# A two-block transformer trunk on one core: where the modulation's products are computed, and how they are spread behind the tiles of the first projection

## The chip, the cores and the metric

The kernel runs on one core of one Trainium2 chip. The metric is the device time of one execution in microseconds (us); three executions of the kernel before gave 1600.56, 1601.52 and 1603.43, so 1601.52 is its median.

## The reference, cut to what matters

Two transformer blocks run over 256 tokens of width 2048, in float32. The part that the change touches is the head of the first block:

- `mod = silu(c) @ w_ada + b_ada`: one row vector of 2048 against a 2048 x 6144 matrix. It is split into shift, scale and gate, of 2048 each.
- `h = rms(x) * (1 + scale) + shift`, then `proj = h @ w_in`, 2048 x 8192.
- Attention and a gated recurrence follow, then `x = x + gate * (y @ w_out)`, and then the second block.

So shift and scale of a stretch of 512 columns of `h` must be known before `w_in` can be multiplied with those columns; gate is needed only at the end of the first block.

## The kernel before, in words

**Modulation.** `w_ada` is cut into tiles of 512 rows x 512 columns, 1 MB each: tile (ng, kg) holds output columns 512 ng and up, and rows 512 kg and up. `ada_tile` (line 368) loads one tile by the SP queue (line 372 or 374) and runs its four chunks of 128 rows (line 375): each chunk multiplies a 128x512 block by a column of `cact` and adds it to an accumulator. A plan of four letters says who does each chunk. "V" is one scalar_tensor_tensor on VectorE (line 382; the first one of an accumulator a tensor_scalar, line 380). "P" is a multiplication on ScalarE into a buffer `pts` of two (line 387), and an addition on GpSimd (line 388; the first one only the multiplication, line 384). After the fourth kg, `ada_sum` (line 393) adds up the 128 partitions of each accumulator by matmuls with ones on TensorE, one set for each accumulator of the plan, and VectorE adds the bias (line 399).

**Order.** `ada_steps` (line 402) is a generator that gives one tile at each step. Of a pair of column groups, one of scale (ng 4 to 7) and one of shift (ng 0 to 3), the tiles alternate. The first pair comes in the front, beside the projection of the memory. The other three pairs come in the first three passes over `w_in`, with `PAIR`: all chunks of the scale group by "P", all of the shift group by "V". The four gate groups (ng 8 to 11) come later with `GATES`: three "V" and one "P" in each tile of the first three groups, each gate group with two accumulators and so two sets of matmuls.

**The passes.** The loop at line 833 goes over four row groups kg of `w_in`, and in each over 12 tiles n of 512 x 512. `tile_mm` (line 141) loads a tile into one of three buffers (`wr`, line 108) and does it in two halves of 256 rows. For each half, ScalarE casts it to `wh` (line 121), VectorE writes the difference to `wl` (line 122, two buffers), and TensorE multiplies (line 166). After the matmuls of a half, `drain` gives out queued work, here mostly one evacuation `part` of an earlier tile: on ScalarE in the first pass (line 632), on VectorE in the others (line 634). After the second half, `post` calls `after` (line 811), which advances the modulation by one tile where n is 0, 1, 2, 4, 5, 6, 8, 9 or 10 (the ninth step is the last sum). After n = 11, `make_h` (line 429) builds the next 512 columns of `h` from the pair: four instructions at line 436 and four at line 438 on VectorE, four at line 437 on ScalarE. Pass kg + 1 multiplies with these columns, so it can't begin before them. In the passes `AHEAD` is 0: a half is multiplied as soon as it is split.

**Gates.** In the fourth pass the modulation is advanced at n = 10 only. After it, the linears of lines 891 to 895 advance it after each tile, in `post` (line 190), while the recurrence (line 747) runs beside them on VectorE, GpSimd, ScalarE and TensorE.

**Queues.** Each engine takes its instructions in order; a scheduler of the language puts them in that order at build time, near the written one but not the same. All loads are issued by SP in order. A load waits until its buffer is free, and the loads behind it wait with it. The tiles of `w_ada` in the passes have two buffers of their own (line 365), used in turn; those of the gates share `wr`.

Of the kernel before, what the change touches and what calls it, by code (L numbers as in the profile page):

```python
# [33 lines left out]
BUDGET = dict(mem=0.3, pass0=0.5, pass3=2.0, gz=1.3, az=1.1, out=0.5, in2=0.1, mla=0.9, o=0.6, ffn=0.1, down=0.3)  # L34


GATES = ("VVVP", "VVVP", "VVVP", "VVVV")
PAIR = ("PPPP", "VVVV")

EARLY = 3  # L40
GSTART = 10
# [19 lines left out]
def trunk_kernel(ctx, tc, a, out):  # L61
# [76 lines left out]
        while jobs:  # L138
            jobs.popleft()()

    def tile_mm(src, kc0, kt, cw, mode, banks, act, first, last, pre=None, post=None):

        raw = load(src, kt, cw)
        n = 2 if mode == "N" else cw // P
        nk = 4 if cw == 256 else 2

        def one(kc, b, hi, lo):
            xh, xl, xx = act(kc0 + kc)  # L150
            hi, lo = hi[:, kc % nk, :], lo[:, kc % nk, :]
            st, sp = first and kc == 0, last and kc == kt - 1
            if mode == "T":
                o = banks[b // 2][:, (b % 2) * T : (b % 2) * T + T]
                s = slice(b * P, b * P + P)
                trip = ((o, hi[:, s], xh), (o, hi[:, s], xl), (o, lo[:, s], xh))
                st = st and b % 2 == 0
            elif mode == "T2":
                s = slice(b * P, b * P + P)
                trip = ((two(banks[b]), hi[:, s], xx), (banks[b][:, :T], lo[:, s], xh))  # L160
            else:
                o = banks[b][:, :cw]
                s = slice(b * P, b * P + P)
                trip = ((o, xh[:, s], hi), (o, xh[:, s], lo), (o, xl[:, s], hi))
            for i, (d, l, r) in enumerate(trip):
                PE.matmul(d, l, r, start=st and i == 0, stop=sp and i == len(trip) - 1, skip_group_check=True)  # L166

        def job(k, hi, lo):
            if k == 0 and pre is not None:
                pre()  # L170
            if not banks:
                banks.extend(bank("mm") for _ in range((cw // P + 1) // 2 if mode == "T" else 2))
            pairs = [(kc, b) for kc in range(k, k + nk) for b in range(n)]
            if last and k + nk == kt:
                pairs.sort(key=lambda p: p[1])
            for kc, b in pairs:
                one(kc, b, hi, lo)
            drain(BUDGET[phase[0]])
            if k + nk == kt and post is not None:
                post()  # L180

        for k in range(0, kt, nk):
            hi, lo = split_w(raw, k, cw, mode)
            submit(lambda k=k, hi=hi, lo=lo: job(k, hi, lo))

    def linear(groups, kgs, act, kt=4, need=None, aside=None, done_loads=None, ahead=None, nkc=99):


        state = [(src, cw, mode, evac, []) for src, cw, mode, evac in groups]

        def post(final, evac, banks):
            if aside is not None:
                next(aside, None)
            if final:
                if done_loads is not None and state[0][3] is evac:
                    done_loads()
                evac(banks)

        for ki, kg in enumerate(kgs):
            if ahead is not None:  # L200
                ahead(kg)
            for gi, (src, cw, mode, evac, banks) in enumerate(state):
                final = ki == len(kgs) - 1
                tile_mm(src(kg), kg * kt, min(kt, nkc - kg * kt), cw, mode, banks, act, ki == 0, final,
                        (lambda kg=kg: need(kg)) if need is not None and gi == 0 else None,
                        lambda final=final, evac=evac, banks=banks: post(final, evac, banks))
# [161 lines left out]
    def ada_tile(ng, kg, accs, plan):  # L368

        raw = ada_buf(ng)  # L370
        if raw is None:
            raw = load(a["w_ada"][ng, kg], 4, 512)
        else:
            SP.dma_start(raw, a["w_ada"][ng, kg].rearrange("p (k c) -> p k c", k=4))
        def chunk(k):
            cc = cact[:, 4 * kg + k : 4 * kg + k + 1]
            first = kg == 0 and plan[k] not in plan[:k]
            if plan[k] == "V":
                if first:
                    V.tensor_scalar(accs[0], raw[:, k, :], cc, None, ALU.mult)  # L380
                else:
                    V.scalar_tensor_tensor(accs[0], raw[:, k, :], cc, accs[0], ALU.mult, ALU.add)  # L382
            elif first:
                S.mul(accs[1], raw[:, k, :], cc)
            else:
                t = tmp([P, 512], "pts")
                S.mul(t, raw[:, k, :], cc)  # L387
                G.tensor_tensor(accs[1], accs[1], t, ALU.add)  # L388

        for k in range(4):  # L390
            chunk(k)

    def ada_sum(ng, accs):
        ps = bank("ax")
# [7 lines left out]
    def ada_steps(ngs, plans):  # L402
# [9 lines left out]
                        if len(set(plan)) == 2 else (tmp([P, 512], "acc", 1) if i == 0 else slot("s8", [P, 512]),) * 2)  # L412
        for kg in range(4):
            for i, ng in enumerate(ngs):
                ada_tile(ng, kg, accs[i], plans[i])
                if kg == 3 and i:
                    yield
                if kg == 3:
                    f = lambda ng=ng, i=i: ada_sum(ng, accs[i][: len(set(plans[i]))])
                    if ng < 8:  # L420
                        f()
                    else:
                        later(0.1, lambda f=f, ng=ng: (f(), done.add(f"g{ng}")), evq)
                yield
# [18 lines left out]
    def front():  # L443
        steps = ada_steps((4, 0), ("VVVV", "VPPP"))
        for i, n in enumerate(FRONT):
            for _ in range(n):
                next(steps, None)
            if 1 <= i <= 4:
                load_x(i - 1)
            if i == 5:  # L450
                spread = token_R(sums[:, 4:8, :], R2, r2)
            if i == 6:
                spread()
            if i == 7:
                make_h(0)
            yield

    S.activation(cact, colr("c"), AF.Silu)
# [349 lines left out]
    gates, xp = gate_steps(), []  # L808
    steps, hgt = [], []

    def after(kg, n, banks, ng, mode, dst, g, fin):
        for i, b in enumerate(banks):
            later(0.6, lambda i=i, b=b: part(kg, ng, mode, dst, g, b, i, fin), evq)
        if n == 0:
            steps.append(ada_steps((4 + kg + 1, kg + 1), PAIR) if kg < 3 else gates)
        if (n % 4 < EARLY and (kg < 3 or n >= GSTART)):
            next(steps[-1], None)
        if kg == 1 and n == 2:
            load_masks()
        if kg == 3 and n == 3:  # L820
# [12 lines left out]
    for kg in range(4):  # L833
        phase[0] = "pass3" if kg == 3 else "pass0"
        for n, (ng, mode, dst, g, fin) in enumerate(first_groups):
            banks = []
            tile_mm(a["w_in"][ng, kg], 4 * kg, 4, 512, mode, banks, acth, True, True,
                    post=lambda kg=kg, n=n, banks=banks, ng=ng, mode=mode, dst=dst, g=g, fin=fin:
                    after(kg, n, banks, ng, mode, dst, g, fin))


# [608 lines left out]
```

## Time and profile before

| | us |
|---|---|
| median of three executions | 1601.52 |
| the profiled execution, its own time | 1603.98 |
| its span, first to last instruction | 1602.2 |
| TensorE matmul busy | 1539.2 (96%) |
| TensorE weight load busy | 1388.4 (87%) |
| VectorE busy | 1159.0 (72%) |
| ScalarE busy | 860.7 (54%) |
| GpSimd busy | 369.3 (23%) |

Times in the trace count from the first instruction. In the rows, PE is the matmul row of TensorE and PEld its weight loads, DVE is VectorE, ACT is ScalarE, POOL is GpSimd and SP the queue that issues loads; L122 is line 122 of the kernel. The four passes over `w_in` lie at 91.5 to 166 us (called pass 0 in the text), 166 to 235 (pass 1), 235 to 304 (pass 2) and 304 to 380 (pass 3); the gates are done between about 370 and 500 us, the last of them near 600. Where two instructions follow each other at once, the second starts some 0.08 us before the printed end of the first; the chain of waits prints the time from start to start.

### The profile page before, as it was taken

Reading aid. Unit: us, or ns where it says so; the run is one execution under the profiler, and the core shown is the slowest. Engines: PE = TensorE matmul, PEld = TensorE weight load, DVE = VectorE, ACT = ScalarE, POOL = GpSimd, SP = SyncE. Lnnn points to the kernel's source line nnn. Section 1 sums busy time; section 2 is a strip of 40 time slices with the busy share of each in tenths; the row PEclk is TensorE's granted clock in tenths of the full one; section 3 lists DMA queues with packets and bytes.
Section 4 is the critical chain, followed back from the end, with each engine's and each line's share of the span. In section 5 each row is a group of like instructions: output and inputs, shape, how many; then the busy total and the mean of one; then the engine's idle time right before and its main releaser. Section 6 shows DMA issues by size and latency. Waiting matters only on the chain.

```text
span 1602.2 us, 24898 instructions
## 1 busy us (share of the span) xinstructions
PE 1539.2 (96%) x9754; PEld 1388.4 (87%) x9754; DVE 1159.0 (72%) x1611; ACT 860.7 (54%) x1254; POOL 369.3 (23%) x363
## 2 busy tenths in 40 slices
PE   5789999999899999999999999999999999999999
PEld 4587888878898999987999888888888888888887
DVE  7777899899997769567667676676676676545444
ACT  6366655564556745367645555555555555333332
POOL 3533435156653011513101211111111111000000
PEclk9899999999999999999999999999999999999999
DMA  9567888553655566444445555555555555556653
GB/s 384 201 260 274 331 315 318 189 183 133 219 199 213 178 248 261 161 164 147 144 141 177 183 201 191 189 205 185 194 201 184 198 196 188 200 191 209 207 189 131
DMA packets 50805, 331.68 MB, mean 207 GB/s; under 512 B 5632, under 2 KB 7936, under 8 KB 13312
## 3 DMA queue, kind: packets, MB, share of 16 engines
q1 hardware_dynamic: 50688, 330.10, 57.4%
q8 instruction: 76, 1.25, 0.3%
q14 instruction: 41, 0.34, 0.1%
HBM read 327.98 MB, written 2.10 MB: 206 GB/s over the span
## 4 chain that ended last, share of the span: by engine, by line
PE 84%; DVE 9%; issue 2%; POOL 2%; ACT 2%; DMA 2%; SPq 0%; DVEq 0%; ACTq 0%; POOLq 0%
PE mm L166 78%; DVE wl L122 4%; DVE acc L382 2%; PE ax L724 1%; DMA wr<-in_w_mem_kv_dram 1%; ACT wh L121 1%; PE ax L397 1%; PE ax L254 1%; PE ax L224 1%; DMA y<-in_w_ada_dram 1%; PE ax L522 1%; POOL acc L388 0%; PE ax L514 0%; DVE y L725 0%; DVE s L314 0%
## 5 line engine op out<-in xcount | busy, mean ns | idle before, releaser
L122 DVE TENSOR_TENSOR wl<-wr,wh 128x1024 fp32r<-128x1024 f32 (+2 forms) x516 | 669.2, 1299 | 338.2 <-PE mm L166 304.7
L121 ACT CAST wh<-wr 128x1024 fp32r<-128x1024 f32 (+2 forms) x516 | 535.1, 1040 | 465.5 <-PE mm L166 387.9
L166 PE MATMUL mm<-h,wh 128*128 128x512 f32 (+1 forms) x2560 | 689.2, 342 | 0.6 <-ACT wh L121 0.6
L166 PE MATMUL mm<-h,wl 128*128 128x256 f32 x1984 | 552.6, 279 | 8.9 <-DVE wl L122 8.8
L166 PEld LDWEIGHTS mm<-h,wh 128*128 128x128 f32 x2560 | 443.7, 190 | 56.3 <-ACT wh L121 1.2
L166 PEld LDWEIGHTS mm<-h,wl 128*128 128x128 f32 x1984 | 375.0, 189 | 11.3 <-DVE wl L122 11.2
L166 PE MATMUL mm<-f,wh 128*128 128x512 f32 x704 | 239.4, 389 | 0.0
L166 PE MATMUL mm<-wh,h 128*128 128x512 f32 (+1 forms) x704 | 218.8, 386 | 0.0
L166 PE MATMUL mm<-f,wl 128*128 128x256 f32 x704 | 194.3, 276 | 0.0
L166 PE MATMUL mm<-y,wh 128*128 128x256 f32 x1024 | 181.8, 281 | 0.0
L166 PEld LDWEIGHTS mm<-f,wh 128*128 128x128 f32 x704 | 132.2, 188 | 27.3
L166 PEld LDWEIGHTS mm<-y,wh 128*128 128x128 f32 x1024 | 155.3, 188 | 0.0
L166 PEld LDWEIGHTS mm<-wh,h 128*128 128x128 f32 x704 | 131.1, 188 | 24.3
L166 PE MATMUL mm<-y,wl 128*128 128x256 f32 x512 | 142.7, 280 | 3.6 <-DVE wl L122 3.6
L166 PE MATMUL mm<-wl,h 128*128 128x512 f32 (+1 forms) x352 | 135.4, 385 | 3.2 <-DVE wl L122 3.2
L166 PEld LDWEIGHTS mm<-f,wl 128*128 128x128 f32 x704 | 132.2, 188 | 0.0
L1288 POOL TENSOR_TENSOR gp<-sg,R 128x256 f32<-128x256 f32 x44 | 36.1, 820 | 314.2 <-DVE sg L1287 314.2
L388 POOL TENSOR_TENSOR acc<-acc,pts 128x512 f32<-128x512 f32 x45 | 75.9, 1686 | 109.9 <-ACT pts L387 107.7
L166 PEld LDWEIGHTS mm<-y,wl 128*128 128x128 f32 x512 | 96.4, 189 | 4.6 <-DVE wl L122 4.4
L166 PEld LDWEIGHTS mm<-wl,h 128*128 128x128 f32 x352 | 66.2, 188 | 17.4 <-DVE wl L122 5.8
L166 PE MATMUL mm<-wh,s 128*128 128x512 f32 x128 | 44.9, 431 | 10.1 <-ACT wh L121 10.1
L634 DVE TENSOR_TENSOR s<-mm,s 128x512 f32<-128x512 f32 x72 | 49.1, 682 | 1.7 <-PE mm L166 1.3
(306 smaller groups left out, 1564.5 us busy)
## 6 DMA issues: line engine op xcount, KB each, us to landing
wr<-in_w_in_dram SPq DMA_DIRECT2D x76, 1024.0 KB, 4.9
wr<-in_w_gate_dram SPq DMA_DIRECT2D x44, 1024.0 KB, 4.8
wr<-in_w_up_dram SPq DMA_DIRECT2D x44, 1024.0 KB, 4.9
wr<-in_w_down_dram SPq DMA_DIRECT2D x40, 1024.0 KB, 4.9
y<-in_w_ada_dram SPq DMA_DIRECT2D x28, 1024.0 KB, 7.0
wr<-in_w_ada_dram SPq DMA_DIRECT2D x16, 1024.0 KB, 4.8
wr<-in_w_out_dram SPq DMA_DIRECT2D x16, 1024.0 KB, 4.8
wr<-in_w_o_dram SPq DMA_DIRECT2D x16, 1024.0 KB, 4.8
```

What stands on the lines that cost most here:

```text
L121: S.copy(hi, raw[:, k : k + n, :])
L122: V.tensor_tensor(lo, raw[:, k : k + n, :], hi.bitcast(F32), ALU.subtract)
L166: PE.matmul(d, l, r, start=st and i == 0, stop=sp and i == len(trip) - 1, skip_group_check=True)
L224: PE.matmul(ps[:, tb * P : tb * P + P], work[:, k, tb * P : tb * P + P], ones, start=k == 0, stop=k == 3, skip_group_check=True)
L254: PE.transpose(ps[:, j * T + tb * P : j * T + tb * P + P], d[:, j, tb * P : tb * P + P], ident)
L382: V.scalar_tensor_tensor(accs[0], raw[:, k, :], cc, accs[0], ALU.mult, ALU.add)
L388: G.tensor_tensor(accs[1], accs[1], t, ALU.add)
L397: PE.matmul(ps[:, j * P : j * P + P], acc[:, j * P : j * P + P], ones, start=i == 0, stop=i == len(accs) - 1, skip_group_check=True)
L522: PE.matmul(po[:, :T], vblk(0), t[:, :T], start=True, stop=False, skip_group_check=True)
L634: V.tensor_tensor(d, b, d, ALU.add)
L724: PE.matmul(ps[:, j, b, :], k2[:, j, s], q2[:, j, s], start=True, stop=True)
L1288: G.tensor_tensor(gp[:, 2:], s, R3, ALU.mult)
```

## The change

All plans become "V": the 48 chunks of ng 5, 6 and 7 and one chunk in each of 12 gate tiles go from ScalarE and GpSimd to VectorE, and the three gate groups have one accumulator. `ada_tile` gives way after its second chunk; in the passes the generator is advanced after each half tile instead of after each tile, so two chunks stand behind each half. In `linear` the generator is advanced twice behind each tile, and the front does twice as many steps at each place: there the order stays.

```diff
-GATES = ("VVVP", "VVVP", "VVVP", "VVVV")
-PAIR = ("PPPP", "VVVV")
+GATES = ("VVVV", "VVVV", "VVVV", "VVVV")
+PAIR = ("VVVV", "VVVV")
...
-    def tile_mm(src, kc0, kt, cw, mode, banks, act, first, last, pre=None, post=None):
+    def tile_mm(src, kc0, kt, cw, mode, banks, act, first, last, pre=None, post=None, mid=None):
...
             if k + nk == kt and post is not None:
                 post()
+            elif mid is not None:
+                mid()
...
             if aside is not None:
                 next(aside, None)
+                next(aside, None)
...
         for k in range(4):
             chunk(k)
+            if k == 1:
+                yield
...
-                ada_tile(ng, kg, accs[i], plans[i])
+                yield from ada_tile(ng, kg, accs[i], plans[i])
                 if kg == 3 and i:
+                    yield
                     yield
...
-            for _ in range(n):
+            for _ in range(2 * n):
...
+    def modulate(kg, n):
+
+        if len(steps) == kg:
+            steps.append(ada_steps((4 + kg + 1, kg + 1), PAIR) if kg < 3 else gates)
+        if n % 4 < EARLY and (kg < 3 or n >= GSTART):
+            next(steps[-1], None)
...
-        if n == 0:
-            steps.append(ada_steps((4 + kg + 1, kg + 1), PAIR) if kg < 3 else gates)
-        if (n % 4 < EARLY and (kg < 3 or n >= GSTART)):
-            next(steps[-1], None)
+        modulate(kg, n)
...
-                    post=lambda kg=kg, n=n, banks=banks, ng=ng, mode=mode, dst=dst, g=g, fin=fin:
+                    mid=lambda kg=kg, n=n: modulate(kg, n), post=lambda kg=kg, n=n, banks=banks, ng=ng, mode=mode, dst=dst, g=g, fin=fin:
```

## Rows read from the trace of the kernel before

**Rows 1.** Busy time by stretch: PE, PEld, DVE, ACT, POOL (instructions); clock, DMA, GB/s
```profile
91.50:166.00 74.50, 69.81 (x399) 60.55 (x400) 53.68 (x60) 50.14 (x71) 25.52 (x18) 0.98 0.73 274
166.00:235.00 69.00, 67.62 (x399) 59.66 (x398) 65.05 (x73) 38.73 (x49) 28.69 (x17) 1.00 0.84 317
235.00:304.00 69.00, 67.42 (x399) 59.61 (x398) 64.22 (x79) 34.20 (x40) 28.18 (x18) 1.00 0.77 280
...
380.00:440.00 60.00, 55.11 (x420) 52.16 (x419) 57.15 (x83) 30.23 (x46) 37.67 (x39) 0.97 0.53 191
```
**Rows 2.** Waits in pass 0, pass 1 and pass 2: us in total, times, longest
```profile
PE mm L166 <- DVE wl L122: 3.4, 4, 1.6
...
PE mm L166 <- DVE wl L122: 1.4, 2, 0.8
...
PE mm L166 <- DVE wl L122: 1.6, 2, 1.2
```
**Rows 3.** Timeline of POOL, ACT and PE in pass 0: start, us, instruction [idle before]
```profile
107.29 6.25 POOL L388 TENSOR_TENSOR acc<-acc,pts 128x512 f32<-128x512 f32 x4 [6.88 <-ACT pts L387]
...
110.84 0.73 ACT L387 ACTIVATE pts<-y,cact 128x512 f32<-128x512 f32 x1 [1.50 <-POOL acc L388]
...
114.68 0.39 PE L166 MATMUL mm<-h,wl 128*128 128x256 f32 x1 [1.62 <-DVE wl L122]
```
**Rows 4.** Instructions by line, whole run: ns min/median/max, first and last start
```profile
L122 DVE TENSOR_TENSOR wl<-wr,wh x516: 807/1226/3361, 10.1 to 1593.0; 128x1024 fp32r<-128x1024 f32 x166, 128x640 fp32r<-128x640 f32 x3, 128x768 fp32r<-128x768 f32 x3
...
L382 DVE SCALAR_TENSOR_TENSOR s<-y,cact,s x46: 735/745/1768, 75.2 to 285.4; 128x512 f32<-128x512 f32 x46
...
L634 DVE TENSOR_TENSOR s<-mm,s x72: 661/682/692, 173.6 to 394.1; 128x512 f32<-128x512 f32 x72
...
L388 POOL TENSOR_TENSOR acc<-acc,pts x45: 1277/1507/2302, 93.4 to 277.4; 128x512 f32<-128x512 f32 x45
```
**Rows 5.** Groups of pass 1 by line and shape: count, busy us, mean ns
```profile
L122 DVE TENSOR_TENSOR wl<-wr,wh 128x1024 fp32r<-128x1024 f32 x24 | 34.7, 1447 | 3.6 <-PE mm L166 2.3 <-issue 0.9 <-ACT pts L387 0.4
```
**Rows 6.** Chain of waits, two stretches: start, us to the next, what
```profile
352.55 2.74 PE mm L166 x12
...
449.78 2.74 PE mm L166 x24
...
235.73 0.87 DVE h L438 x2
236.60 1.14 DVE wl L122
237.74 0.40 DVE s L380
...
240.53 0.60 DVE s L634
241.13 0.67 DVE s L382
...
288.63 0.89 PE ax L397 x8
```
**Rows 7.** Landing of the `w_ada` loads of line 374, and a wait in pass 1
```profile
DMA to landing us min/median/max: 4.7/7.1/17.5
...
ACT pts L387 <- DMA y<-in_w_ada_dram: 1.4, 1, 1.4
```
**Rows 8.** Gates: timeline of DVE and POOL, and the chain of waits
```profile
402.19 1.77 DVE L382 SCALAR_TENSOR_TENSOR acc<-wr,cact,acc 128x512 f32<-128x512 f32 x1
...
401.95 1.47 POOL L388 TENSOR_TENSOR y<-y,pts 128x512 f32<-128x512 f32 x1
...
424.41 1.78 PE ax L397 x16
```
**Rows 9.** Timeline of ACT at the turn from pass 0 to pass 1
```profile
161.23 0.72 ACT L384 ACTIVATE acc<-y,cact 128x512 f32<-128x512 f32 x1 [0.81 <-DMA y<-in_w_ada_dram]
...
163.41 1.71 ACT L437 ACTIVATE h<-y,modT 128x256 fp32r<-128x256 f32 x4
```

More of the change, by code (lines that the diff above doesn't have):

```diff
@@ L455, in front @@
                 make_h(0)
+            yield
             yield
```

## The prediction, written before the changed kernel was run

> **What bounds the kernel now.** I read the busy time by stretch first, then the waits of each pass, then the timeline around one stall, then the lines by themselves. TensorE is busy nearly all the time, and the passes are where the change acts: they take 74.5, 69 and 69 us [rows 1]. What TensorE must do in a pass follows from the chain of waits: a half tile takes it 2.74 us, whether the tile is of the form with 24 short matmuls or the one with 12 long ones, and a sum over partitions of one accumulator takes 0.89 [rows 6]. A pass has 24 halves and two sums: 24 x 2.74 + 2 x 0.89 = 67.5 us. That is the floor; pass 0 lies 7.0 above it, passes 1 and 2 1.5 each.
>
> What lifts a pass over the floor is mostly `wl` arriving late: TensorE waits for line 122 for 3.4, 1.4 and 1.6 us [rows 2]. One such stall shows why. Four additions on GpSimd run from 107.29 to 113.5; ScalarE, which has two `pts` buffers, waits 1.50 us for them before the last product, and its next cast `wh` stands behind that product; then `wl` is late, and TensorE waits 1.62 us at 114.68 [rows 3]. A second loss is in VectorE itself: line 122 has a median of 1226 ns and goes up to 3361, line 382 has 745 and goes up to 1768, while line 634, of the same engine in the same passes but with one operand in PSUM, never leaves 661 to 692 [rows 4]. The additions of GpSimd are stretched too, from 1277 ns to 2302 [rows 4]. So instructions of VectorE with two operands in SBUF and the additions of GpSimd hold each other up. In pass 1 this lifts the mean of line 122 to 1447 ns [rows 5].
>
> **The change, part by part.** *Removed from ScalarE and GpSimd:* in each pass 16 products and 15 additions, so the stall of [rows 3] loses its cause. ScalarE is at 50.1, 38.7 and 34.2 us of the passes [rows 1]; that it gets less is worth nothing by itself.
>
> *Added to VectorE:* 16 chunks a pass, one as line 380 and 15 as line 382: 0.40 + 15 x 0.67 = 10.5 us [rows 6]. Given back: the stretch. In pass 1, 24 x (1.447 - 1.226) = 5.3 us at line 122 [rows 4, 5]; that pass standing for three, some 16 us of relief against 31 us of new work.
>
> The Trainium skill, "SBUF — State Buffer", section "Who interferes with whom", has a two-input VectorE instruction and a GpSimd instruction that reads SBUF exclude each other for a whole instruction. If each of the 45 additions held VectorE for its whole 1.28 us, moving it for 0.67 would be a gain of 27 us on VectorE instead of a loss of 15. The trace agrees with the rule's direction and not with that bound, because an addition also falls where VectorE is idle or reads PSUM; I go by the rows.
>
> *VectorE's load after.* By start-to-start times, a pass needs 24 x 1.14 for `wl`, 24 x 0.60 for the parts, 2 x 0.40 + 30 x 0.67 for 32 chunks, and 8 x 0.43 for `make_h` [rows 6]: 27.4 + 14.4 + 20.9 + 3.4 = 66.1 us. Against the floor of 67.5 no slack is left, but it is not over it. Pass 0 has its parts on ScalarE: 51.7 us.
>
> *Two chunks behind each half.* In passes 1 and 2 a tile with modulation costs VectorE 2 x 1.14 + 2 x 0.60 + 4 x 0.67 = 6.16 us against 5.48 of TensorE: 0.68 us is lost per tile, 2.0 in three tiles running, and the tile without modulation (3.48) gives 2.0 back. Two `wl` buffers let VectorE lead by 2.74 - 1.14 = 1.6 us, so TensorE waits 0.4 us at the end of each three, twice a pass: 0.8. With all four chunks behind the tile, the `wl` after them would come 1.14 + 2.68 + 0.60 + 1.14 = 5.56 us after a freed buffer, when 5.48 are there: nearly the same wait, at every tile. The halving is worth about that.
>
> *The loads.* Their order on SP is unchanged, since both places lie between the loads of two `w_in` tiles. But a `w_ada` tile is now wanted at the half: where three tiles run together, from the last chunk that frees a buffer to the first chunk that wants its next content it was 2 x 5.48 - 3 x 0.67 = 8.9 us and is 2 x 5.48 - 2.74 - 0.67 = 7.5. A load lands in 4.7 to 17.5 us, median 7.1; before, ScalarE waited once, 1.4 us [rows 7]. VectorE now waits instead of ScalarE, and the next `wl` is queued behind it; TensorE waits for that. I take 0.5 us a pass; the bounds are 0 and two waits of 10 us.
>
> *Pass 0.* Nothing is late on VectorE, with 51.7 us of load, so what GpSimd caused goes. The one stall shown is 1.6 us [rows 3]; the whole excess is 7.0, part of which is the end of the memory's keys. Between them I take 4.0, nearer to the 3.4 of [rows 2].
>
> *Passes 1 and 2.* The excess of 1.5 each goes, and 0.8 + 0.5 comes back: 0.2 gained each, 0.4 together; bounds, 1.5 each gained, or what the rivals below cost.
>
> *Gates.* VectorE is the busiest there, 57.2 us of 60 [rows 1]. Twelve chunks come, 12 x 0.67 = 8.0 us. Nine additions go, and each that falls on a chunk costs VectorE about 1.0: at 401.95 an addition of 1.47 us turns the chunk of 402.19 into 1.77 us [rows 8], against 0.745 [rows 4]. If all nine hit, 9 us; I take 6.5, leaving 1.5 us more on VectorE. TensorE's sums of three gate groups are halved, from 1.78 us [rows 8] to 0.89: 2.7 us gained, all on the chain. Together -1.2; bounds -3.7 and +5.3.
>
> Sum: -4.0 - 0.4 - 1.2 = -5.6 us. The profiled execution took 1603.98 us, so its like would take 1598.4; it stands 2.5 us above the median of 1601.52, and from that median the sum gives 1595.9, rounded to 1596.0.
>
> **The rivals.** *VectorE becomes the bound (slower).* If instructions cost their printed median instead of the start-to-start time [rows 4], the load of a pass is 24 x 1.226 + 24 x 0.682 + 30 x 0.745 + 0.8 + 3.4 = 72.4 us, 3.4 over today's 69 in passes 1 and 2; with the gates 1.5 worse than now and 4.0 saved in pass 0, that is +4.3: 1605.8. It decides from a load of about 69 us; between 66 and 69 it eats only the gain, near 1600. For it: 65.1 and 64.2 us are busy already [rows 1]. Against: those sums hold the stretch.
>
> *The load at the half (slower).* Six places, two a pass, have 7.5 us. If loads there land in 10, VectorE stands 2.5 us at each, 15 us in all less the 1.5 counted: +7.9, 1609.4. For: the median of 7.1 is close and the maximum far. Against: before, one short wait in a pass.
>
> *No relief (slower).* If the stretch is not GpSimd's doing, passes 1 and 2 need 65.05 + 10.5 and 64.22 + 10.5 us on VectorE, 6.6 and 5.7 over 69, and the gates 8.0 - 2.7: +17.6, 1619. Line 634 speaks against it. The Trainium skill, "Perfetto Trace Analysis", section "Optimizing Scalar/DVE Operations", holds that with VectorE saturated, handing some work to ScalarE or even GpSimd may pay; undoing it would then cost this much. The same section adds that between VectorE and GpSimd it might not help, which [rows 4] bear out.
>
> *The chunks are not spread as written.* The scheduler moves instructions: the first product of pass 1's modulation runs at 161.23, before the line 437 of `make_h` at 163.41 that is written ahead of it [rows 9]. If chunks end up in fours, the waits at the tiles' ends stay, some 0.1 to 0.2 us at 16 tiles: 1599.
>
> **How the numbers follow.** Forecast 0.50, bound on VectorE 0.21, load at the half 0.12, no relief 0.04, not spread 0.13. Forecast's own range, from the bounds of pass 0 and the gates: 1592 to 1600. The slow end of the range takes in VectorE as bound and leaves out most of the load's case: 1592 to 1607. About 0.2%, 3.2 us, is what a measurement of this kernel tells from no change, so faster means under 1598.3 and slower over 1604.7. Faster: most of the forecast and part of the last rival, 0.51. Same: the rest of these and half of VectorE's case, 0.28. Slower: 0.21.
>
> **What would show it.** Right: lines 387 and 388 gone after pass 0's start; line 122 in the passes at a mean near 1.23 us, line 382 near 0.745; passes near 70.5, 68.8 and 68.8 us; in pass 0 no wait of a cast behind GpSimd; the sums of gates at 0.89. Wrong: VectorE busy to the end of passes 1 and 2 with TensorE waiting for line 122 over 3 us in each (bound on VectorE); waits of line 380 or 382 for `w_ada` loads (load at the half); line 122 still at 1.4 (no relief).

## The result, and the profile of the changed kernel

The changed kernel takes 1591.1 us, the median of four executions (1587.9 to 1594.0); the kernel before, run beside it, takes 1602.5 (1600.6 to 1603.8). The ratio is 0.9928, with a 95% interval of 0.9912 to 0.9943. So it is faster by some 11 us, twice the 5.6 that were forecast, and lies 0.9 us below the range. The two profiled executions differ by 10.0 us, 1603.98 to 1593.98, and it is these 10.0 that the traces can place.

First the busy time by stretch, passes 0, 1 and 2 of the changed kernel, with the columns of [rows 1]:

```profile
91.30:160.00 68.70, 67.59 (x401) 59.66 (x402) 58.49 (x80) 40.66 (x54) 1.75 (x1) 1.00 0.82 306
160.00:228.00 68.00, 68.00 (x402) 60.47 (x401) 66.16 (x91) 27.76 (x30) 0.00 (x0) 1.00 0.87 323
228.00:296.00 68.00, 68.00 (x402) 60.47 (x401) 65.79 (x90) 26.99 (x28) 4.32 (x5) 1.00 0.76 284
```

TensorE is busy for all 68.00 us of passes 1 and 2; before it was idle 1.4 and 1.6 us of 69 [rows 1]. VectorE has 66.16 and 65.79 us of work in them, only 1.1 and 1.6 more than before, although 10.5 us of chunks came to it. GpSimd does nothing in pass 1.

The chain of waits of the changed kernel from 96.67 us, near pass 0's start (start, us to the next piece, what):

```profile
96.67 46.21 PE mm L166 x285
142.88 0.89 PE ax L402 x8
143.77 10.90 PE mm L166 x48
154.67 0.89 PE ax L402 x8
155.56 55.30 PE mm L166 x336
...
222.64 0.89 PE ax L402 x8
223.53 55.30 PE mm L166 x336
...
291.50 33.42 PE mm L166 x239
```

From 96.67 to 324.9 us nothing but TensorE ends last. The reader can take the true floor of a pass from it: 155.56 to 223.53 and 223.53 to 291.50 are 67.97 us each, where the prediction had 67.5. (A half tile takes (67.97 - 1.78) / 24 = 2.758 us on average, and its form does matter: the first eight halves of pass 1, with 24 short matmuls, take 22.61 us by the lines shown further below, 2.83 each; the other sixteen 2.72. The prediction had 2.74 for both.)

The lines that answer to [rows 2] and [rows 7], from the waits of pass 0 of the changed kernel (us in total, times, longest); passes 1 and 2 have no wait of TensorE at all:

```profile
PE mm L166 <- DVE wl L122: 1.8, 2, 1.1
...
DVE acc L383 <- DMA y<-in_w_ada_dram: 0.3, 1, 0.3
```

Both waits of the first line lie at pass 0's start, before 96.7. The second is VectorE's only wait for a load in the three passes. Then the durations of line 122 in the three passes alone, in the kernel before (first fence) and in the changed one (second fence, with the chunks and the parts of the whole run behind it, which answer to [rows 4]; ns min/median/max, first and last start):

```profile
L122 DVE TENSOR_TENSOR wl<-wr,wh x72: 1209/1225/2321, 96.9 to 303.9; 128x1024 fp32r<-128x1024 f32 x72
```

```profile
L122 DVE TENSOR_TENSOR wl<-wr,wh x72: 1211/1221/1229, 95.4 to 294.0; 128x1024 fp32r<-128x1024 f32 x72
...
L385 DVE SCALAR_TENSOR_TENSOR s<-y,cact,s x46: 739/745/753, 75.0 to 281.2; 128x512 f32<-128x512 f32 x46
...
L641 DVE TENSOR_TENSOR s<-mm,s x72: 657/682/692, 165.3 to 384.0; 128x512 f32<-128x512 f32 x72
```

The longest `wl` has fallen from 2321 ns to 1229, the longest chunk of `s` from 1768 [rows 4] to 753. The medians stay, and so does the line that reads PSUM. The stretch went with GpSimd's additions; runs 2 and 4 below bring them back, and it with them.

**Where the 10.0 us went.** The first matmul of each sum over partitions marks the same work in both kernels. It starts at 78.3 us (front's first sum), 161.0 (pass 0's last), 230.7, 300.3 and 618.4 (the last gate) before, and at 78.1, 154.5, 222.5, 290.5 and 608.6 after:

| from the mark before to | before | after | moved | forecast |
|---|---|---|---|---|
| front's first sum | 78.3 | 78.1 | -0.2 | |
| pass 0's last sum | 82.7 | 76.4 | -6.3 | -4.0 |
| pass 1's last sum | 69.7 | 68.0 | -1.7 | -0.2 |
| pass 2's last sum | 69.6 | 68.0 | -1.6 | -0.2 |
| last gate's sum | 318.1 | 318.1 | 0.0 | -1.2 |
| end of the span | 983.8 | 983.6 | -0.2 | |

The marks are read to 0.1 us, so a row can be off by that much.

**Pass 0 taken apart.** In the kernel before, the timeline of TensorE has these idle times in pass 0 beside the 1.62 us of [rows 3] (start, us, instruction, idle before and its releaser), and VectorE this group at its start:

```profile
94.87 0.52 PE L254 MATMUL ax<-ident,memk 128*128 128x128 f32 x2 [0.71 <-DVE memk L327]
96.27 1.33 PE L254 MATMUL ax<-ident,memk 128*128 128x128 f32 x5 [0.88 <-DVE memk L327]
...
132.19 0.50 PE L166 MATMUL mm<-wl,h 128*128 128x512 f32 x1 [0.88 <-DVE wl L122]
149.02 1.16 PE L397 MATMUL ax<-ones,acc 128*128 128x128 f32 x8 [0.44 <-POOL acc L388]
...
93.26 3.74 DVE L327 TENSOR_SCALAR memk<-memk,ssm 128x128 f32<-128x128 f32 x8 [1.16 <-POOL ssm L211]
```

and these are stretches of it by windows:

```profile
95.00:99.00 4.00, 2.96 (x13) 2.27 (x14) 4.00 (x8) 2.05 (x4) 1.13 (x1) 0.70 0.00 0
99.00:103.00 4.00, 4.00 (x32) 4.00 (x32) 3.93 (x5) 2.60 (x4) 1.34 (x1) 0.87 0.68 260
...
99.00:100.00 1.00, 1.00 (x6) 1.00 (x6) 1.00 (x2) 0.87 (x1) 0.93 (x1) 0.50 0.05 16
...
101.00:102.00 1.00, 1.00 (x11) 1.00 (x10) 0.96 (x2) 0.22 (x2) 0.00 (x0) 1.00 1.01 426
...
98.20:161.00 62.80, 59.86 (x343) 52.23 (x344) 44.78 (x43) 40.70 (x56) 19.99 (x13) 0.99 0.79 296
```

In the changed kernel the same group of VectorE, and the same stretch of matmuls, read:

```profile
93.16 1.66 DVE L330 TENSOR_SCALAR memk<-memk,ssm 128x128 f32<-128x128 f32 x8 [1.53 <-POOL ssm L214]
```

```profile
96.70:154.60 57.90, 57.90 (x342) 51.31 (x343) 49.39 (x61) 32.38 (x41) 0.00 (x0) 1.00 0.88 329
```

The eight multiplications that end the memory's keys take 3.74 us where two additions of GpSimd fall on them, and 1.66 without: the steady row of matmuls begins 19.9 us after the front's sum (98.2 - 78.3) before and 18.6 after it (96.7 - 78.1), 1.3 less. From there to the sum it is 62.8 against 57.9, 4.9 less: 62.80 - 59.86 = 2.9 us of idle TensorE (the 1.62, 0.88 and 0.44 above), and 59.86 - 57.90 = 2.0 us of slower matmuls. About half of the 2.0 is the clock: before, the granted clock is 0.70 and 0.87 in the two stretches from 95 to 103 us, so it is partly on the lower of its two levels there, right behind the waits for `memk`. By single microseconds it is 0.50 up to 100, where 6 matmuls run in a microsecond in place of 11; from 98.2 to 100 that costs some 1.0 us. In the changed kernel's pass 0 the clock is 1.00. The other half, some 0.9, stands at the edges of the three stalls, where the matmuls just before and just behind the idle time follow each other more slowly than elsewhere, at a clock of 1.00. 1.3 + 2.9 + 2.0 = 6.2; with their edges the three stalls cost 3.8.

### The profile page after: what moved, and what is told of

Same layout as the page of the kernel before. It is cut to its first block, busy times and chain, and to the rows that moved or that the text cites. A ratio compares the mean times of both kernels' runs of the same rounds, so it can differ in the third digit from the quotient of the medians.

```text
span 1592.2 us, 24722 instructions
## 1 busy us (share of the span) xinstructions
PE 1534.7 (96%) x9730; PEld 1384.7 (87%) x9730; DVE 1165.7 (73%) x1671; ACT 823.0 (52%) x1194; POOL 280.5 (18%) x309
## 4 chain that ended last, share of the span: by engine, by line
PE 85%; DVE 9%; issue 2%; POOL 2%; ACT 2%; DMA 1%; SPq 0%; DVEq 0%; ACTq 0%; POOLq 0%
PE mm L166 80%; DVE wl L122 3%; DVE acc L385 2%; DMA wr<-in_w_mem_kv_dram 1%; ACT wh L121 1%; PE ax L731 1%; DVE y L732 1%; PE ax L227 1%; PE ax L529 1%; PE ax L402 1%; DVE R L704 0%; DVE y L712 0%; PE ax L521 0%; PE ax L257 0%; DVE s L317 0%
## 5 line engine op out<-in xcount | busy, mean ns | idle before, releaser
L122 DVE TENSOR_TENSOR wl<-wr,wh 128x1024 fp32r<-128x1024 f32 (+2 forms) x516 | 652.5, 1266 | 321.9 <-PE mm L166 298.9
L166 PEld LDWEIGHTS mm<-h,wl 128*128 128x128 f32 x1984 | 373.4, 188 | 13.5 <-DVE wl L122 13.4
L385 DVE SCALAR_TENSOR_TENSOR acc<-wr,cact,acc 128x512 f32<-128x512 f32 x60 | 49.9, 831 | 0.3
```

What stands on the lines that cost most here:

```text
L122: V.tensor_tensor(lo, raw[:, k : k + n, :], hi.bitcast(F32), ALU.subtract)
```

## The experiments

**1. Whole tiles, all on VectorE.** The kernel before with nothing but the plans changed:

```diff
-GATES = ("VVVP", "VVVP", "VVVP", "VVVV")
-PAIR = ("PPPP", "VVVV")
+GATES = ("VVVV", "VVVV", "VVVV", "VVVV")
+PAIR = ("VVVV", "VVVV")
```

> The kernel before with the plans of the change (all chunks on VectorE) but still four chunks behind a whole tile. Theory GpSimd (the additions on GpSimd are the cause of the stalls, and how the chunks are spread hardly matters): no wait behind GpSimd in the three passes, line 122 at a mean near 1.22 us, passes near 68 to 68.5 us, nearly the whole gain: -9 to -11 us, 1591 to 1594. Rival spreading (four chunks in front of a split make it late): VectorE as busy as in the changed kernel (66 us of 68) but TensorE waits for line 122 behind each of the 8 tiles with modulation, 0.5 us or more at each, 4 us a pass and 12 us in all, so the gain is gone: 1600 to 1604.

Measured: 1591.95 us, 0.9928 of the kernel before (0.9913 to 0.9942). That is the whole gain, without the halving, as the first of the two expectations had it. Pass 1 of this run, by windows and by VectorE's lines:

```profile
156.00:224.00 68.00, 68.00 (x402) 60.47 (x401) 66.30 (x91) 28.09 (x31) 0.00 (x0) 1.00 0.87 323
```

```profile
L122 DVE TENSOR_TENSOR wl<-wr,wh 128x1024 fp32r<-128x1024 f32 x25 | 30.5, 1220 | 1.5 <-PE mm L166 1.0 <-issue 0.2
```

It can't be told from the changed kernel, and the order shows why: VectorE's instructions of passes 1 and 2 stand in the two traces in the same sequence but for a few exchanged neighbours. The scheduler mostly puts one or two chunks behind a `wl`, rarely three, in either way of writing.

**2. Half tiles, old plans.** The changed kernel with the two plans put back:

```diff
-GATES = ("VVVV", "VVVV", "VVVV", "VVVV")
-PAIR = ("VVVV", "VVVV")
+GATES = ("VVVP", "VVVP", "VVVP", "VVVV")
+PAIR = ("PPPP", "VVVV")
```

> The changed kernel with the plans of before: chunks in twos behind each half, but half of them still by ScalarE and GpSimd. Theory GpSimd: line 122 stays at a mean of 1.40 us or more in the passes, casts still wait behind GpSimd, passes as before (74, 69.7, 69.6 us): within 2 us of the kernel before. Rival spreading: two chunks at a time are what frees TensorE, passes near 68 us: -8 us or more.

Measured: 1602.1 us, 0.9995 (0.9984 to 1.0007). The halving alone gives nothing. Pass 1 by VectorE's lines has the stretch back:

```profile
L122 DVE TENSOR_TENSOR wl<-wr,wh 128x1024 fp32r<-128x1024 f32 x24 | 34.7, 1447 | 2.0 <-PE mm L166 1.2 <-ACT pts L390 0.4 <-issue 0.4
```

**3. Only the gates as before.**

```diff
-GATES = ("VVVV", "VVVV", "VVVV", "VVVV")
+GATES = ("VVVP", "VVVP", "VVVP", "VVVV")
```

> The changed kernel with the old plans for the gates only (one chunk in four of three gate groups by ScalarE and GpSimd, two accumulators). By the comparison of the two traces the gain lies in the three passes (-6.3, -1.8, -1.6 us) and the gates give next to nothing: then this is within 2 us of the changed kernel, 1590 to 1593. Rival (the forecast's term for the gates, -1.2, or more): 1.2 to 3 us slower than the changed kernel, and TensorE's sums of 1.78 us are back on the chain.

Measured: 1591.9 us, 0.9931 (0.9916 to 0.9947), the same as the changed kernel. So no gain of the gates' part can be told. A gain of the 1.2 us that were forecast isn't excluded either: both intervals reach some 2.4 us to each side, and in this run's own trace the stretch from pass 2's last sum to the last gate's takes 322.0 us, against 318.1 to 318.7 in the other traces with the old gates (the kernel before, runs 2 and 5) and 316.5 to 319.3 with the new ones (the changed kernel, runs 1, 4, 6, 8 and 9). Put with runs 1 and 2, all of the gain that can be told is in `PAIR`.

**4. The additions without the products.** To the changed kernel, 15 additions of GpSimd a pass, of the shape of those removed, whose result nobody reads; ScalarE has no part in them:

```diff
+    dead = []
...
+                if ng in (5, 6, 7):
+                    if first:
+                        dead[:] = [tmp([P, 512], "pts")]
+                        G.memset(dead[0], 0.0)
+                    else:
+                        G.tensor_tensor(dead[0], dead[0], raw[:, k, :], ALU.add)
```

> The changed kernel with 15 additions of 128x512 on GpSimd in each of the three passes whose result nobody uses (one beside each chunk of groups 5, 6 and 7, reading the same loaded block); ScalarE has no part in them. Theory both (VectorE and GpSimd hold each other up, and that alone is enough): line 122 back to a mean of 1.35 us or more, VectorE's need in passes 1 and 2 is 66 + 6 = 72 us, so these passes take 71 to 73 us and the whole is 6 to 10 us slower than the changed kernel: 1597 to 1601. Rival (the stall of ScalarE's casts behind GpSimd was the cause, the stretch of VectorE harmless): under 2 us slower than the changed kernel, passes still near 68 us.

Measured: 1619.24 us, 1.0097 (1.0081 to 1.0113). Against 0.9928 that is 27 us for 45 additions: the direction that was expected, at nearly three times the upper end of the 6 to 10 us. Pass 1 (80 us) by windows, and by the lines of VectorE and of GpSimd:

```profile
166.00:246.00 80.00, 71.17 (x406) 60.12 (x405) 79.81 (x95) 29.25 (x34) 24.53 (x15) 1.00 0.75 279
```

```profile
L122 DVE TENSOR_TENSOR wl<-wr,wh 128x1024 fp32r<-128x1024 f32 x25 | 35.1, 1404 | 0.0
...
L387 DVE SCALAR_TENSOR_TENSOR acc<-y,cact,acc 128x512 f32<-128x512 f32 x14 | 13.5, 962 | 0.0
L387 DVE SCALAR_TENSOR_TENSOR s<-y,cact,s 128x512 f32<-128x512 f32 x15 | 13.0, 866 | 0.1
```

```profile
L393 POOL TENSOR_TENSOR pts<-pts,y 128x512 f32<-128x512 f32 x15 | 24.5, 1636 | 48.2 <-DMA y<-in_w_ada_dram 47.3
```

VectorE is never idle now, 79.81 us of 80, so all of the stretch is on the path. From sum to sum the pass takes 80.4 us, 12.4 more than in the changed kernel: 0.83 us for each of the 15 additions. A chunk done by VectorE itself costs it 0.67 [rows 6]. So, with VectorE full, handing the addition to GpSimd takes more of VectorE's time than doing the whole chunk there. In the kernel before it took less, and VectorE had idle time to lose there: the mean `wl` of [rows 5] was as long as here, but 4 us of the 69 were free [rows 1]. (Passes 0 and 2 are 7.8 and 10.6 us longer than in the changed kernel. In pass 2 the additions also stand behind a wait of GpSimd for another load, and the loads of `w_ada` behind the additions, so only pass 1 prices them.)

**5. More room for the products.** The rival was that ScalarE's order does it: two `pts` buffers, a product that waits for an addition, and the cast `wh` behind it [rows 3]. The kernel before, with its products in five buffers:

```diff
-                t = tmp([P, 512], "pts")
+                if ng in (5, 6, 7):
+                    npt[0] += 1
+                    t = spare[0][:, 1 + npt[0] % 3] if npt[0] % 4 else tmp([P, 512], "pts")
+                else:
+                    t = tmp([P, 512], "pts")
```

> The kernel before, where ScalarE's products of groups 5, 6 and 7 go to five buffers in place of two, so that ScalarE no longer waits for GpSimd's additions before its next cast; the additions stay. Theory stretch (VectorE and GpSimd holding each other up is most of the loss): line 122 still at 1.40 us or more, and only what the late casts cost in pass 0 comes back: -1 to -4 us, 1599 to 1602. Rival order (casts standing behind products that wait for GpSimd are most of the loss): pass 0 near 77 us from the front's sum to its own last sum (82.7 before, 76.4 changed), passes 1 and 2 near 68: -7 us or more, 1596 or less.

Measured: 1601.8 us, 0.9995 (0.9982 to 1.0007): no difference. Pass 0 by windows, and one of VectorE's lines in it:

```profile
91.00:166.00 75.00, 71.30 (x398) 62.19 (x399) 56.55 (x61) 51.65 (x75) 29.44 (x19) 0.95 0.74 275
```

```profile
L327 DVE TENSOR_SCALAR memk<-memk,ssm 128x128 f32<-128x128 f32 x8 | 4.7, 663 | 1.2 <-POOL ssm L211 1.2
```

and `wl` in its pass 1:

```profile
L122 DVE TENSOR_TENSOR wl<-wr,wh 128x1024 fp32r<-128x1024 f32 x24 | 34.0, 1415 | 2.3 <-issue 0.8 <-ACT pts L393 0.6 <-PE mm L166 0.5
```

TensorE is idle less (75.00 - 71.30 = 3.7 us of pass 0, against 4.7 [rows 1]), so the queue behind the products was one of the stalls. But three additions instead of two now fall on the `memk` multiplications (663 ns each against 282 in the changed kernel), the granted clock of the pass is 0.95, and the time is the same. The order on ScalarE is a way in which the additions hurt, not the whole of it. Passes 1 and 2 say so too: from sum to sum they take 68.1 and 70.4 us (69.7 and 69.6 before, 69.5 and 68.4 in run 2). Pass 1 is all but at the floor although its `wl` is stretched to a mean of 1415 ns. So the stretch alone doesn't make a pass longer; it does where it leaves TensorE without the next split half, and how the 1.5 us of a pass divide between the stretch and the order on ScalarE is not shown. With all chunks on VectorE both passes take 67.97 us in each trace, except where work was added to VectorE or additions to GpSimd (runs 4 and 7). Products on ScalarE with additions on VectorE were not tried.

**6. The front as well.** What is left of the mixed plans is in the front, three chunks of each shift tile on ScalarE and GpSimd. The changed kernel with

```diff
-        steps = ada_steps((4, 0), ("VVVV", "VPPP"))
+        steps = ada_steps((4, 0), ("VVVV", "VVVV"))
```

> The changed kernel with the front's shift group on VectorE alone as well (VPPP becomes VVVV: 12 chunks more, 11 additions of GpSimd less, 4 sums of TensorE less, before 90 us). Theory stretch: an addition costs VectorE 0.6 to 0.9 us, a chunk 0.67, so VectorE is no worse off, and the chain of the front, which runs through 5.1 us of GpSimd's additions around 43 to 49 us, loses these: 1 to 4 us faster than the changed kernel. Rival (the front is bound by the first loads and by VectorE's splits, 67.7 us of 91 busy): no change, or up to 3 us slower.

Measured: 1583.39 us, 0.9874 (0.9859 to 0.9889), 0.0054 or some 8.7 us below the changed kernel; 1 to 4 were expected. The front's first sum starts at 68.6 us instead of 78.1 (the same front has it at 74.6 to 76.0 in runs 1 to 4, 7 and 8).

**7. How much room VectorE has left.** The changed kernel with one more chunk for each of the eight tiles of a pass, whose result nobody reads:

```diff
+                if ng in (1, 2, 3, 5, 6, 7) and k == 3:
+                    if not dead or dead[0] != kg0(ng):
+                        dead[:] = [kg0(ng), tmp([P, 512], "pts")]
+                        V.tensor_scalar(dead[1], raw[:, k, :], cc, None, ALU.mult)
+                    else:
+                        V.scalar_tensor_tensor(dead[1], raw[:, k, :], cc, dead[1], ALU.mult, ALU.add)
```

> The changed kernel with one chunk more on VectorE for each of the 24 modulation tiles of the passes, into an accumulator nobody reads (8 x 0.67 = 5.4 us a pass; the buffer of the tile is not held longer). VectorE's load becomes 66.2 + 5.4 = 71.6 us in passes 1 and 2, against 68.0 of TensorE. Theory levelled (VectorE's work is spread so evenly that TensorE waits only where the load of a whole pass is over its own): pass 0 unchanged, passes 1 and 2 near 71.6: +7 us on the changed kernel, 1597 to 1600. Rival (VectorE has hidden slack in a pass, its parts can slip into the next): under +4 us.

Measured: 1595.43 us, 0.9957 (0.9942 to 0.9971), 0.0029 or 4.6 us above the changed kernel, between the two expectations (7, and under 4). Passes 1 and 2 by windows, and a wait in the second:

```profile
155.00:224.00 69.00, 68.61 (x403) 60.66 (x402) 68.40 (x95) 27.73 (x30) 0.34 (x1) 1.00 0.85 324
224.00:296.00 72.00, 69.55 (x403) 60.44 (x403) 71.16 (x100) 27.53 (x31) 5.14 (x5) 1.00 0.74 265
...
PE mm L166 <- ACT wh L121: 2.2, 3, 0.9
```

Eight chunks are 0.40 + 7 x 0.67 = 5.1 us, which puts VectorE's load at some 71 us against the floor of 68. Pass 1 pays 1.1 of it from sum to sum and pass 2 3.7 (the last sum of both passes comes in two parts here, and the second part is the mark). VectorE is busy for 68.40 us of 69 and 71.16 of 72: it falls behind in the one pass, and most of the debt is paid in the other. How it reaches TensorE there isn't settled, for 2.2 of TensorE's 2.45 us of idle time in the second stretch are put down to ScalarE's casts. The changed kernel, with VectorE busy for 66.16 of 67.97 us, has 1.8 us left before the load alone would make VectorE the bound.

**8. GpSimd work that reads nothing.** The Trainium skill, "SBUF — State Buffer", section "Who interferes with whom", has a two-input VectorE instruction contend only with a GpSimd instruction that reads SBUF, and instructions such as `tensor_scalar`, which can go in a mode with two ports, with any; in such a mode the one that issues second blocks entirely, for the whole of the other's instruction. The changed kernel with 32 memsets a pass in place of run 4's additions:

```diff
+                if ng in (5, 6, 7):
+                    if first:
+                        dead[:] = [tmp([P, 512], "pts")]
+                    for _ in range(2):
+                        G.memset(dead[0], 0.0)
```

> The changed kernel with 32 memsets of 128x512 on GpSimd in each of the three passes (0.53 us each, 17 us a pass, into a tile that nobody reads): GpSimd works as long as with the additions, but only writes. Theory reads (it is the second input of VectorE and the reads of GpSimd that exclude each other): line 122 stays at 1.22 us, passes at 68.0, no change against the changed kernel. Rival (any work of GpSimd in SBUF holds up VectorE): line 122 at 1.3 us or more, passes 1 and 2 slower by 3 us or more each.

Measured: 1612.83 us, 1.0067 (1.0046 to 1.0088). The scheduler ran most of the memsets in one row at pass 0's start. The timelines of VectorE and of GpSimd, then VectorE's lines from 113 us to the end of that row, then the durations of the `memk` line:

```profile
90.44 22.47 DVE L330 TENSOR_SCALAR memk<-memk,ssm 128x128 f32<-128x128 f32 x8 [1.62 <-POOL ssm L214]
...
90.35 38.35 POOL L392 MEMSET pts<- 128x512 f32 x74
```

```profile
L122 DVE TENSOR_TENSOR wl<-wr,wh 128x1024 fp32r<-128x1024 f32 x7 | 8.5, 1221 | 1.0 <-PE mm L166 0.9
L387 DVE SCALAR_TENSOR_TENSOR acc<-y,cact,acc 128x512 f32<-128x512 f32 x7 | 5.2, 744 | 0.1
```

```profile
L330 DVE TENSOR_SCALAR memk<-memk,ssm x8: 498/620/20572, 90.4 to 112.4; 128x128 f32<-128x128 f32 x8
```

Measured against the changed kernel that is 0.0139, some 22 us, which neither expectation had. Both halves of the rule show. Seven `wl` and seven chunks run beside the memsets at 1221 and 744 ns, as if GpSimd were idle, where run 4's additions made them 1404 and 962. And one `tensor_scalar` of 128x128, 282 ns in the changed kernel, takes 20.57 us: it stands until the row of memsets lets it in. The whole loss is there; passes 1 and 2 take 68.0 us as in the changed kernel. So what stretches VectorE's two-input instructions goes with the additions' reading, not with GpSimd being busy; a one-input instruction of VectorE can be held up by GpSimd's writing alone. Beside the two-input ones this was seen in some 15 us of pass 0, since the scheduler left no memset for passes 1 and 2.

**9 to 12. The same move elsewhere.** Run 6, and in addition: in run 9 the additions to the sums of squares (six of 128x1024 in the front, three later); in run 10 the products of the recurrence's levels; in run 11 these and the levels' differences; in run 12 all of them. Each is the letter G turned into V:

```diff
-            G.tensor_tensor(acc, acc, work, ALU.add)
+            V.tensor_tensor(acc, acc, work, ALU.add)
...
-            G.tensor_tensor(snd(k2), snd(k), fst(d), ALU.mult)
+            V.tensor_tensor(snd(k2), snd(k), fst(d), ALU.mult)
...
-            G.tensor_tensor(fst(k2), fst(k), fst(d), ALU.mult)
+            V.tensor_tensor(fst(k2), fst(k), fst(d), ALU.mult)
...
-                G.tensor_tensor(fst(d), ref, snd(bb), ALU.subtract)
+                V.tensor_tensor(fst(d), ref, snd(bb), ALU.subtract)
...
-                G.tensor_tensor(fst(d), ref, fst(bb), ALU.subtract)
+                V.tensor_tensor(fst(d), ref, fst(bb), ALU.subtract)
```

> The all-VectorE front (the run before with 0.9874) with the sums of squares also added on VectorE: 12 additions of 128x1024 in all, 6 of them in the front, 2.4 us each on GpSimd, about 1.15 on VectorE. Theory (an addition of GpSimd costs VectorE about as much as the addition itself, so moving it is free, and it lands sooner): 1 to 4 us faster than that front, 1579 to 1582. Rival (VectorE is busy 64 of the front's 80 us and its queue is what the front waits for): 2 to 7 us slower.

> The all-VectorE front, with the 32 products of the recurrence that GpSimd does (128x256, 0.98 us each there; VectorE's own of that size follow each other at 0.33 us) moved to VectorE. Does the lesson of the passes hold where VectorE is the busiest engine (58 us of 60)? Theory (each of them costs VectorE 0.4 us or more while GpSimd does it): 10.6 us of work against some 13 of relief, 0 to 4 us faster than that front. Rival (they mostly fall beside work with an operand in PSUM, so nothing is given back): 5 to 10 us slower.

> As the run with the products on VectorE, and the 28 differences of the recurrence's levels (128x256, 0.97 us or more on GpSimd) there too. Theory: no change or up to 4 us faster than with the products alone. Rival: 5 to 10 us slower again, since VectorE's queue is what the recurrence waits for.

> All the moves from GpSimd to VectorE at once: the front's modulation chunks, the additions to the sum of squares, the recurrence's products and its level differences. If each gain comes from a stretch of its own, they add: the squares gave 9.9 us on the run with the front alone (1583.39 to 1573.45) and the products and differences 3.9 (1583.39 to 1579.49), so 1568 to 1571 us. Rival: the two share VectorE's queue in the stages where both lie, VectorE is there the engine that ends last, and the products and differences give nothing more or take some back: 1573 to 1577 us.

| run | us | ratio to before | 95% interval |
|---|---|---|---|
| 6, front | 1583.39 | 0.9874 | 0.9859 to 0.9889 |
| 9, + squares | 1573.45 | 0.9825 | 0.9810 to 0.9839 |
| 10, + products | 1581.01 | 0.9871 | 0.9857 to 0.9886 |
| 11, + products, differences | 1579.49 | 0.9864 | 0.9848 to 0.9881 |
| 12, all | 1571.42 | 0.9800 | 0.9786 to 0.9813 |

The runs stand beside different executions of the kernel before, so the ratios are compared. The squares give 0.0049, 7.8 us, on top of the front, where 1 to 4 were expected. Products and differences give 0.0010, within the interval, so nothing is shown of them alone; run 12 against run 9 is 0.0025, 4 us, with intervals that just overlap. It lies a little above the sum of gains that its expectation named first and below the rival's span. Run 12 is the fastest kernel of this study, 2% below the kernel before. What the front and the squares did is one line of waits in the first 100 us, here of the changed kernel, run 6 and run 9:

```profile
PE mm L166 <- DVE wl L122: 18.2, 7, 8.7
```

```profile
PE mm L166 <- DVE wl L122: 12.8, 7, 5.8
```

```profile
PE mm L166 <- DVE wl L122: 4.3, 5, 2.2
```

The front's first sum starts at 78.1, 68.6 and 59.8 us, and TensorE waits less for `wl`. In the changed kernel's first 92 us, 5.6% of the chain of waits lie on line 391's additions of GpSimd and 3.6% on line 250's, and these left. How much of the gain is that, and how much a VectorE that is held up less, was not taken apart. (An addition to the squares has a median of 2405 ns on GpSimd and 1218 on VectorE.)

## Why the prediction was right and wrong, point by point

**The mechanism was right.** The forecast was that the two engines hold each other up and that the relief nearly pays for the new work. The relief in pass 1 is 24 x (1.447 - 1.220) = 5.4 us at line 122, forecast 5.3; VectorE's load is 66.16 us, forecast 66.1. The relief as a whole was larger than the 5.3 "given back" in the text: 10.5 us of work came and the busy time grew by 1.1 and 1.6, so some 9 us came back a pass, the rest of it at the chunks and the other lines that read SBUF. The sum of the load had that in it without saying so, since it took every instruction at its unstretched price. Run 4 puts additions back alone, and more than the gain is lost; run 2 puts the whole plan back, and the gain is gone. "No relief" is refuted: work came back to a VectorE that was busy 94% of the pass, and the pass became shorter. The section of the Trainium skill that the prediction named beside it ("Perfetto Trace Analysis", "Optimizing Scalar/DVE Operations") has both sides, that a saturated VectorE may hand work to GpSimd and that between these two it might not help; in this case the second held.

**The sizes.** Against the forecast of -5.6 the two traces give -10.0. Passes 1 and 2 are 2.9 of the 4.4 between them, pass 0 is 2.3, the gates take 1.2 off, and front and end give 0.4. That the total is about twice the forecast is the sum of misses in both directions.

**The step that failed is the one on passes 1 and 2**: "the excess of 1.5 each goes, and 0.8 + 0.5 comes back". The excess went (1.7 and 1.6), and nothing came back. Two costs had been set against it.

- *"TensorE waits 0.4 us at the end of each three, twice a pass: 0.8."* This held each tile's four chunks to its own two halves. Pass 1's first tile begins behind pass 0's last one, where the form of the matmuls changes, and the form changes again after four tiles (first fence: start, us, instruction of TensorE in the changed kernel). So `wl` at 175.24 and at 178.07 are the two of n = 3, the tile without modulation (second fence: VectorE):

```profile
160.62 0.39 PE L166 MATMUL mm<-wh,h 128*128 128x512 f32 x1
160.85 0.40 PE L166 MATMUL mm<-h,wh 128*128 128x256 f32 x2
...
183.46 0.40 PE L166 MATMUL mm<-wh,h 128*128 128x512 f32 x1
```

```profile
175.24 1.23 DVE L122 TENSOR_TENSOR wl<-wr,wh 128x1024 fp32r<-128x1024 f32 x1 [0.19 <-issue]
...
178.07 1.23 DVE L122 TENSOR_TENSOR wl<-wr,wh 128x1024 fp32r<-128x1024 f32 x1 [0.78 <-PE mm L166]
179.21 0.68 DVE L641 TENSOR_TENSOR s<-mm,s 128x512 f32<-128x512 f32 x1
179.81 1.53 DVE L385 SCALAR_TENSOR_TENSOR s<-y,cact,s 128x512 f32<-128x512 f32 x2
```

  Behind the second of them run two chunks of the next tile, n = 4, ahead of where they are written. Counted through the pass, the `wl` of n = 0 to 2 have nine chunks behind them in place of twelve, and those of n = 4 to 6 nine: 9 x 0.67 + 6 x (1.14 + 0.60) = 16.5 us, which is what TensorE takes for six halves (6 x 2.758). The tiles without modulation take the others, n = 7 one each way and the last tile of pass 0 three of pass 1's first. So VectorE does not fall behind in three tiles running; at 178.07 it waits for TensorE. The rival that the chunks "are not spread as written" came true, and for the good: its own price was worked out as if the written order were the better one. Run 1 shows that the written halves are not what spreads them.
- *"I take 0.5 us a pass"* for loads wanted at the half. VectorE waited for a load once in three passes, 0.3 us.

**Pass 0 was mis-sized**: -4.0 forecast, -6.3 measured. The three stalls behind GpSimd, 2.9 us idle and 3.8 with their edges, are near the 4.0. Left out were the 1.3 us at the memory's keys, for which the prediction had no price ("part of which is the end of the memory's keys" was put down as staying), and some 1.0 us of lower clock behind them. Line 327 is a one-input instruction, and the sum counted only two-input ones as held up.

**The gates' -1.2 was not seen**: the marks of the table give 0.0 and run 3 no difference, though neither could exclude a gain of that size. In the kernel before the three sums are on the chain of waits, as the prediction had it (1.78, 1.78 and 2.05 us); in the changed kernel only the last is, with 0.91. But the chain from there on is another: over 130 us of the gates the matmuls of line 166 go from 30.3% of it to 17.8%, VectorE's line 122 from 9.2% to 13.5% and its chunks (line 382, now 385) from 11.5% to 13.3%. So what failed is that the 2.7 us were counted as won because the sums lay on the chain; where they went, VectorE and the recurrence end last instead.

**The range** had its low end at 1592, "from the bounds of pass 0 and the gates", without the working. Those bounds together, 7.0 and 3.7 us beside the 0.4 of passes 1 and 2, give 1601.52 - 11.1 = 1590.4, which would have held the result; with the prediction's own bounds for passes 1 and 2 (1.5 gained in each) it is 1587.8.

**The rivals.** VectorE as bound did not come, but was near: its busy time is 1.8 us under TensorE's in a pass, and run 7, with 5.1 us more, is slower. The load at the half did not come.

## What to carry to other kernels

Before an engine is given work to unload VectorE, look at what the helper's instructions do to VectorE's own: compare an instruction's minimum, median and maximum, and one that reads PSUM as a control. Here, with VectorE full, one addition on GpSimd made the pass 0.83 us longer, more than the 0.67 of doing the whole chunk on VectorE, and taking such work back helped in the passes, in the front and at the squares, although VectorE was the busier engine each time. And where a scheduler orders the instructions, estimate waits over a group of tiles with its lead and its slack, not tile by tile as the loops are written.

## What was not expected of the hardware

- A `tensor_scalar` of 128x128 waited 20.57 us for a row of 74 memsets on GpSimd (run 8). It wasn't held for the length of one instruction of GpSimd, about half a microsecond, as the section named in run 8 would have it, but for some forty of them.
- The lower granted clock in pass 0 (0.70 and 0.87 in two stretches of 4 us) is in the kernel before, behind two short waits of TensorE for `memk`, and in runs 2, 4 and 5, which have GpSimd's additions there (0.98, 0.98 and 0.95 over the pass); it is in neither the changed kernel nor run 1 (1.00). TensorE is idle for about 1.1 us between 95 and 97 in the changed kernel too, and its clock stays at 1.00; between 94 and 97 in the kernel before it is idle for some 1.6. That the waits cause it was not tried by itself.
